# A bias table of 23 rows a head written by one transfer, decay read back two steps behind its store, and empty steps between gate and state steps

## The chip, the cores and the metric

The kernel runs on one core of a Trainium2 chip. The metric is the device time of one execution in microseconds (us), the median of several. The engines are TensorE (PE in the profile), VectorE (DVE), ScalarE (ACT), GpSimd (POOL) and SyncE (SP), which here only issues DMAs. Each engine works through its own instructions in order. DMAs are issued by SP and, for stores of projections, by ScalarE.

## The reference

One layer of a hybrid encoder for two groups of requests that share weights: a prompt of 2048 tokens and 8 samples of 16 tokens each. With D = 1024, 8 attention heads of 64 and 4 memory heads of 128:

```python
h = rms_norm(x, norm_g[0])
z = h @ w_in
qa, ka, va, qb, kb, vb, ob, ib, fb = jnp.split(z, IN_SPLITS, axis=-1)
...
idx = jnp.clip(q_pos[:, None] - k_pos[None, :], -REL_CLIP, REL_CLIP) + REL_CLIP
s = s + rel_table[:, idx]                 # chunk-band attention
...
b = jnp.cumsum(lf, axis=-1)               # mLSTM block of 64 tokens
m_t = jnp.maximum(b + m_prev, jnp.max(d_mat, axis=-1))
decay = jnp.exp(b[..., -1] + m_prev - m_new)
c_new = decay[..., None, None] * c_prev + jnp.einsum('bhs,bhsd,bhse->bhde', w_s, k, v)
...
x = x + rms_norm(jnp.concatenate([att, mlstm_out], axis=-1) @ w_out, norm_g[1])
x = x + rms_norm(conv_ffn(rms_norm(x, norm_g[2])), norm_g[3])
```

The bias of attention depends on the distance of query and key alone, so one row of 767 numbers per head holds all that is needed; the row of a query is that row shifted by one.

## The kernel before

All products run in float32 as three passes: each operand is split into a high and a low part, and `mm3` (L95, L96, L97) adds high by high and the two mixed products. A cast on ScalarE makes the high part, a subtraction on VectorE the low one.

The program has these stages, by time in the trace. Until about 1040 us the projection by w_in runs on TensorE, group by group: qk and qb (queries and keys, transposed, stored by L247), va and vo (values, by rows). The copies L232 and L234 on ScalarE take a finished accumulator out of PSUM, and TensorE needs them before it uses the accumulator again. Beside it run two side streams, attention (`att_stream`) and the memory heads (`mem_stream`). From about 1040 to 1300 us comes the product with w_out (`project`; wo is w_out scaled by gatt, L956). Then comes the FFN in a form with fewer products: up-projections (uec, ua, ub), convolution and gate, down-projections (dn and dnm with the halves wdh and wdl of weights and gh and gl of the gated activations). The down stage at about 2175 to 2300 us (names with 1_) has the preparation of rows of h2 interleaved.

A side stream is a `Pipe` of units. A unit is a Python generator that emits instructions up to its next `yield`; the two numbers of a yield are estimates of TensorE and VectorE time. `Pipe.step` starts one new unit and lets every live unit advance by one yield. `pump` is called between the matmuls of a projection and takes up to two such steps, turn and turn about between the pipes, as long as VectorE's estimated share is under 0.615 of the clock. `bubble()` is a unit with no instructions: a step in which only the units already live advance. So a `yield 0.0, 0.0` inside a unit puts distance between its two sides, and a bubble puts distance between two units.

What is emitted is then ordered anew by a scheduler, which simulates a timeline and may move instructions of one engine past each other where data allow it; only what stands in `keep_in_program_order` stays in its order against others of that kind. Tiles come from pools with a fixed number of buffers, and a load into a buffer waits until the last reader of the former content is done. DMAs share eight semaphores, so an issue waits until the DMA eight before it has landed.

The parts that the change touches:

- `build_bias` (L299): a row of 767 numbers for each head (ext) is written to DRAM, and from it the table relrow, in DRAM too, is filled (L310). `load_head` (L333) reads a tile nb of 128 shifted rows for each head and every second key group by `bias_src`; `queries` (L838) reads 16 shifted rows for the samples. A tile is read with a row step of SQ - 1 (SQ is 767), so row p starts p elements earlier.
- `load_head` also loads queries and keys of one head (qraw L342, kraw L345) and casts them (L350, L354).
- `prep_prompt` (L555, once for each half of the prompt) and `prep_sample` (L599) work out the gates: cumulative sums, maxima, and a pack pk of weights. They store the maxima (md, L590; mds, L631) and the decays (dd, L591; dds, L632) to DRAM and read the decays back spread over 128 partitions (dec, L593; decs, L634).
- `mlstm` (L665) loads pairs of chunks (mb from md, L672) and works through them; `mlstm_sample` (L734) takes 8 samples' states in four batches of two for each head: load cs (L777), matmuls cus (L789, L790), update, store (L795). cs has two buffers.
- `attention_sample` (L827) loads cached keys and values in pieces (skr L855, svr L905) through a pool of three raw buffers, casts them (skh L860, svh L909) and subtracts (skl L861, svl L910) for the products ss and sot.

Of the kernel before, what the change touches and what calls it, by code (L numbers as in the profile page):

```python
# [17 lines left out]
P = 128  # L18
# [26 lines left out]
def hymba_step(ctx: ExitStack, tc: tile.TileContext, I: dict, O: dict):  # L45
# [14 lines left out]
    def ps_sm(name):  # L60
        return psum.tile([P, 512], F32, tag="sm", name=name)

    def dt_(shape, name):
        return dram.tile(shape, F32, tag=name, name=name)
# [99 lines left out]
    def bubble():  # L164
        return iter([])
# [119 lines left out]
                    nc.scalar.dma_start(out[s - 3][:, 0 if s == 4 else t % 4, :], stage[:, :256])  # L285


    relrow = dt_([HA, P, SQ], "relrow")

    def raw_tile(name):  # L290
        return pa.tile([P, LS], F32, tag="raw", name=name, bufs=3)
# [7 lines left out]
    def build_bias():  # L299
        ext = dt_([HA, SQ], "ext")  # L300

        def unit():
            far, near = raw_tile("relf")[:HA, :383], rel[0]
            nc.vector.tensor_scalar(near, near, -1.0, None, op0=ALU.mult)
            nc.vector.tensor_copy(far, near[:, 0:1].broadcast_to([HA, 383]))
            nc.sync.dma_start(ext[:, 383:SQ], near)
            nc.sync.dma_start(ext[:, 0:383], far)
            yield 0.0, 0.75
            for h in range(HA):
                tc.keep_in_program_order(nc.sync.dma_start(relrow[h], ext[h:h + 1, :].broadcast_to([P, SQ])))  # L310
                yield 0.0, 0.0
                if h % 2:
                    yield 0.0, 0.0

        yield unit()
        yield FLUSH

    def bias_src(h, rows, cols):
        base = relrow[h]
        return bass.AP(base.tensor, base.offset + 127, [[SQ - 1, rows], [1, cols]])  # L320


    vhl = {}
# [231 lines left out]
    def prep_prompt(half):  # L555
        n = 8
        ig, lf, nlf = log_gates(1 + 8 * half, n, f"p{half}")
        f2 = lambda t: t.rearrange("p c h -> p (c h)")
        yield 0.3, 0.8
        a, b = cum_rows(f2(ig), f2(lf), f2(nlf), 32, tri, f"p{half}")  # L560
        ca = pm.tile([P, P], F32, tag="kw", name=f"cm{half}", bufs=2)[:32, :]
        nc.vector.tensor_tensor_scan(ca, a, a, NEG, op0=ALU.max, op1=ALU.max)
        yield 0.3, 0.4
        rt = ps_sm(f"rt{half}")
        transpose(rt[0:1, 0:32], ca[:, P - 1:P], 32)
        transpose(rt[0:1, 32:64], b[:, P - 1:P], 32)
        row = pm.tile([1, 2, n, HB], F32, tag="rowl", name=f"rowl{half}", bufs=1)
        nc.vector.tensor_copy(row.rearrange("p a c h -> p (a c h)"), rt[0:1, 0:64])
        o = 8 * half
        for h in range(HB):  # L570
            nc.vector.tensor_tensor_scan(mrow[:, o + 1:o + 9, h], row[:, 0, :, h], row[:, 1, :, h],
                                         mrow[:, o:o + 1, h], op0=ALU.max, op1=ALU.add)
        yield 0.3, 0.5
        mp = ps_sm(f"mp{half}")
        transpose(mp[0:32, 0:1], mrow[:, o:o + 8, :].rearrange("p c h -> p (c h)"), 1)
        mprev = small.tile([32, 1], F32, tag="mprev", name=f"mprev{half}")
        nc.vector.tensor_copy(mprev, mp[0:32, 0:1])
        yield 0.3, 0.8
        pk = pm.tile([P, P], F32, tag="kw", name=f"pk{half}", bufs=2)
        nc.vector.tensor_scalar(ca, ca, mprev, None, op0=ALU.max)  # L580
        nml = small.tile([32, 1], F32, tag="nml", name=f"nml{half}")
        nc.vector.tensor_scalar(nml, ca[:, P - 1:P], -1.0, None, op0=ALU.mult)
        nc.vector.tensor_copy(pk[0:32, :], a)
        nc.scalar.activation(pk[32:64, :], ca, AF.Exp, bias=mprev, scale=-1.0)
        nc.vector.tensor_tensor(b, b, ca, op=ALU.add)
        nc.scalar.activation(pk[64:96, :], b, AF.Exp, scale=-1.0)
        nc.scalar.activation(pk[96:128, :], a, AF.Exp, bias=nml)
        md = dt_([32, P], f"md{half}")
        dd = dt_([32, 1], f"dd{half}")
        nc.sync.dma_start(md, ca)  # L590
        nc.sync.dma_start(dd, pk[32:64, P - 1:P])  # L591
        dec = pm.tile([P, n, HB], F32, tag="dec", name=f"dec{half}", bufs=1)
        nc.sync.dma_start(dec, dd.rearrange("(c h) o -> o c h", c=n).broadcast_to([P, n, HB]))  # L593
        yield 0.0, 0.8
        cols = pack_columns(pk, "p")
        stab[half] = (md, dec, cols)
        yield 0.3, 0.8

    def prep_sample():  # L599
        ig, lf, nlf = log_gates(0, 1, "s")  # L600
# [6 lines left out]
        f2 = lambda t: t.rearrange("p c h -> p (c h)")  # L607
        a, b = cum_rows(f2(ig), f2(lf), f2(nlf), HB, trib, "s")
        yield 0.3, 0.8
        ms = small.tile([HB, DB], F32, tag="mss", name="mss")  # L610
        nc.sync.dma_start(ms, I["state_m"])
        ca = pm.tile([P, P], F32, tag="kw", name="cms", bufs=2)[:HB, :]
# [18 lines left out]
        nc.sync.dma_start(md, ca)  # L631
        nc.sync.dma_start(dd, v3(pk[32:32 + HB, :])[:, :, DS - 1])  # L632
        dec = pm.tile([P, HB, DB], F32, tag="decs", name="decs", bufs=1)
        nc.sync.dma_start(dec, dd.unsqueeze(0).broadcast_to([P, HB, DB]))  # L634
        yield 0.0, 0.8
        cols = pack_columns(pk, "s")
        stab["s"] = (md, dec, cols)
        yield 0.3, 0.8


    def finish_heads(num, enm, og, h, nch, dst, name):
# [92 lines left out]
    def mlstm_sample(h):  # L734
# [72 lines left out]
            yield bubble()  # L807
        for bp in range(DB // 2):
            yield batches(bp)
        yield finish()  # L810
        yield FLUSH

# [1075 lines left out]
```

## Time and profile before

| | us |
|---|---|
| median of 3 runs (2784.17 to 2784.3) | 2784.17 |
| the profiled execution | 2787.38 |
| its span | 2785.7 |

| engine | busy, share of the span |
|---|---|
| TensorE, matmuls | 97% |
| TensorE, weight loads | 91% |
| VectorE | 70% |
| ScalarE | 51% |
| GpSimd | 16% |

The mean granted clock of TensorE is 0.994 of full speed. In rows of the trace an instruction stands with its start, its duration, its engine, its line and the tiles it writes and reads; in square brackets is how long its engine stood idle before it and what ended that. SPq and ACTq are DMA issues of SP and ScalarE. In a table by stretches come the stretch, its length, the busy time and count of TensorE's matmuls and weight loads, VectorE, ScalarE and GpSimd, then the granted clock, the busy share of the 16 DMA engines and GB/s. A line of waits has the total, the number and the longest.

### The profile page before, as it was taken

To read this page: it belongs to the slowest core of one execution; us is meant where nothing else is said; L and a number is where in the kernel's file an instruction comes from. 1 tells how busy PE (TensorE), PEld (TensorE's weight loads), DVE (VectorE), ACT (ScalarE), POOL (GpSimd) and SP (SyncE) were. 2 spreads that over 40 slices of the span, in tenths; PEclk is the share of its full clock that TensorE was granted. 3 is DMA by queue.
4 is the path that set the end of the run, shared out by engine and by line. 5 is a ranking of instruction groups with operands and counts; after the bars stand their busy time and mean duration, and the time that the engine had idled before them with its cause. 6 is when DMAs were issued, how large, how long until landed. Compare 5 with 4: busy or idle time off the path is not lost.

```text
span 2785.7 us, 47226 instructions
## 1 busy us (share of the span) xinstructions
PE 2710.7 (97%) x16488; PEld 2536.9 (91%) x16488; DVE 1937.1 (70%) x3562; ACT 1422.1 (51%) x2871; POOL 445.9 (16%) x876
## 2 busy tenths in 40 slices
PE   7999999999999999999999999999999899999998
PEld 7899999998899998878999998799999778999877
DVE  5344455656456668766999988658888786888865
ACT  4355555635356666543554455445545565555543
POOL 1000010212000002244211110111111221222221
PEclk9999999999999999999999999999999999999999
DMA  5544355556555455355644459855555796555595
GB/s 182 158 122 133 104 180 160 169 156 213 157 170 149 143 171 177 111 178 179 217 169 169 167 167 323 295 174 170 177 171 171 252 344 223 169 176 182 177 320 191
DMA packets 334317, 516.35 MB, mean 185 GB/s; under 512 B 57122, under 2 KB 162558, under 8 KB 333950
## 3 DMA queue, kind: packets, MB, share of 16 engines
q1 hardware_dynamic: 295486, 479.49, 53.1%
q10 hardware_dynamic: 38592, 33.83, 3.6%
q8 instruction: 130, 2.13, 0.3%
q14 instruction: 109, 0.89, 0.1%
HBM read 371.61 MB, written 144.72 MB: 185 GB/s over the span
## 4 chain that ended last, share of the span: by engine, by line
PE 50%; DVE 4%; DMA 3%; issue 1%; POOL 1%; ACT 1%; SPq 0%; DVEq 0%; POOLq 0%; ACTq 0%
PE uec L95 6%; PE uec L96 6%; PE uec L97 6%; PE dn L97 3%; PE dn L95 3%; PE dn L96 3%; PE ua L97 3%; PE ua L96 3%; PE ua L95 3%; PE dnm L97 2%; PE dnm L95 2%; PE dnm L96 2%; PE wo L95 2%; PE wo L96 2%; PE wo L97 2%
## 5 line engine op out<-in xcount | busy, mean ns | idle before, releaser
L95 PE MATMUL uec<-B,wuh 128*128 128x384 f32 (+1 forms) x720 | 234.5, 328 | 3.1 <-DVE uu L1490 1.8
L96 PE MATMUL uec<-B,wuh 128*128 128x384 f32 (+1 forms) x720 | 235.1, 327 | 0.0
L97 PE MATMUL uec<-B,wul 128*128 128x384 f32 (+1 forms) x720 | 234.2, 327 | 0.0
L1283 ACT CAST wuh<-wu 128x512 fp32r<-128x512 f32 x255 | 141.7, 617 | 113.6 <-PE uec L96 102.8
L95 PE MATMUL dn<-wdh,gh 128*128 128x512 f32 x444 | 175.4, 395 | 5.6 <-ACT gh L1283 3.0
L96 PE MATMUL dn<-wdl,gh 128*128 128x512 f32 x444 | 175.7, 396 | 0.0
L1284 DVE TENSOR_TENSOR wul<-wu,wuh 128x512 fp32r<-128x512 f32 x255 | 165.1, 683 | 3.3 <-DMA x2d<-mx 3.3
L97 PE MATMUL dn<-wdh,gl 128*128 128x512 f32 x444 | 165.7, 399 | 0.8 <-DVE gl L1284 0.8
L401 DVE CUSTOM_DVE_ANT_0 tmp<-s,nb 128x640 f32<-128x640 f32 (+4 forms) x128 | 94.4, 737 | 97.7 <-PE s L391 95.8
L95 PE MATMUL vo<-wi_h,hT_c 128*128 128x256 f32 x544 | 155.9, 287 | 0.7 <-DVE mt L201 0.6
L97 PE MATMUL vo<-wi_h,hT_c 128*128 128x256 f32 x544 | 156.1, 287 | 0.0
L96 PE MATMUL vo<-wi_l,hT_c 128*128 128x256 f32 x544 | 155.4, 286 | 0.0
L95 PEld LDWEIGHTS uec<-B,wuh 128*128 128x128 f32 x720 | 134.9, 188 | 5.3 <-DVE uu L1490 2.4
L95 PE MATMUL qk<-hT_c,wi_h 128*128 128x384 f32 (+1 forms) x384 | 129.0, 336 | 6.9 <-ACT qk_st L232 4.2
L96 PEld LDWEIGHTS uec<-B,wuh 128*128 128x128 f32 x720 | 135.3, 188 | 0.2
L97 PEld LDWEIGHTS uec<-B,wul 128*128 128x128 f32 x720 | 135.1, 188 | 0.0
L414 DVE TENSOR_TENSOR ptl<-pt,pth 128x640 fp32r<-128x640 f32 (+4 forms) x128 | 93.6, 737 | 57.3 <-ACT pth L413 56.2
L1283 ACT CAST gh<-gr 128x768 fp32r<-128x768 f32 (+3 forms) x92 | 65.1, 719 | 132.0 <-PE dn L96 111.1
L402 ACT ACTIVATE tmp<-tmp,mn 128x640 f32<-128x640 f32 (+4 forms) x128 | 97.6, 763 | 64.7 <-DVE mn L401 62.2
L96 PE MATMUL qk<-hT_c,wi_h 128*128 128x384 f32 (+1 forms) x384 | 128.3, 334 | 0.0
L97 PE MATMUL qk<-hT_c,wi_l 128*128 128x384 f32 (+1 forms) x384 | 128.0, 333 | 0.0
L96 PE MATMUL qb<-hT_c,wi_h 128*128 128x384 f32 (+1 forms) x384 | 127.8, 333 | 0.0
(440 smaller groups left out, 8987.6 us busy)
## 6 DMA issues: line engine op xcount, KB each, us to landing
wu<-in_w_up SPq DMA_DIRECT2D x220, 256.0 KB, 3.7
wu<-wsd SPq DMA_DIRECT2D x176, 256.0 KB, 3.5
wdr<-in_w_down SPq DMA_DIRECT2D x121, 256.0 KB, 5.5
wi_raw<-in_w_in SPq DMA_DIRECT2D x52, 512.0 KB, 4.4
wsd<-ws SPq DMA_DIRECT2D x88, 256.0 KB, 3.0
gr<-gd SPq DMA_DIRECT2D x39, 384.0 KB, 4.2
kraw<-kTd SPq DMA_DIRECT2D x112, 128.0 KB, 3.1
gr<-gd SPq DMA_DIRECT2D x39, 320.0 KB, 5.2
```

The lines of the kernel that those rows point to most:

```text
L95: nc.tensor.matmul(out, ah, bh, start=start, stop=False, skip_group_check=onto)
L96: nc.tensor.matmul(out, ah, bl, start=False, stop=False, skip_group_check=onto)
L97: nc.tensor.matmul(out, al, bh, start=False, stop=stop, skip_group_check=onto)
L401: nc.vector.tensor_tensor_reduce(o_, s_, b_, 1.0, 3e38, ALU.add, ALU.min, accum_out=mn)
L402: nc.scalar.activation(tmp[:, :n], tmp[:, :n], AF.Exp, bias=mn, scale=-1.0, accum_out=rsum[:, i % 4, hh:hh + 1])
L414: nc.vector.tensor_tensor(s.ptl[:, sl, qc], ptv, s.pth[:, sl, qc], op=ALU.subtract)
L1283: nc.scalar.copy(h, r)
L1284: nc.vector.tensor_tensor(l, r, h, op=ALU.subtract)
```

## The change

The table relrow gets 16 + 128/16 - 1 = 23 equal rows a head in place of 128, written by one transfer for all heads. A bias tile of 128 rows is read as 8 groups of 16 rows: inside a group a row starts one element earlier than the one above, and a group starts one table row less 16 elements later, so the values are the same. The steps of `build_bias` fall from one for each transfer and four empty ones to one. The read-backs of decay move to the end of the gate preparation, two yields and some behind their stores, and are kept in program order. Empty yields follow the yields of `prep_prompt` and most of those of `prep_sample`, and a bubble follows each of the four state batches of a head.

```diff
-    relrow = dt_([HA, P, SQ], "relrow")
+    REL_ROWS = 16 + P // 16 - 1
+    relrow = dt_([HA, REL_ROWS, SQ], "relrow")
...
             yield 0.0, 0.75
-            for h in range(HA):
-                tc.keep_in_program_order(nc.sync.dma_start(relrow[h], ext[h:h + 1, :].broadcast_to([P, SQ])))
-                yield 0.0, 0.0
-                if h % 2:
-                    yield 0.0, 0.0
+            tc.keep_in_program_order(
+                nc.sync.dma_start(relrow, ext.unsqueeze(1).broadcast_to([HA, REL_ROWS, SQ])))
+            yield 0.0, 0.0
...
         base = relrow[h]
-        return bass.AP(base.tensor, base.offset + 127, [[SQ - 1, rows], [1, cols]])
+        step = [[SQ - 1, rows]] if rows <= 16 else [[SQ - 16, rows // 16], [SQ - 1, 16]]
+        return bass.AP(base.tensor, base.offset + 127, step + [[1, cols]])
...
         yield 0.3, 0.8
+        yield 0.0, 0.0
         a, b = cum_rows(f2(ig), f2(lf), f2(nlf), 32, tri, f"p{half}")
...
         nc.sync.dma_start(dd, pk[32:64, P - 1:P])
         dec = pm.tile([P, n, HB], F32, tag="dec", name=f"dec{half}", bufs=1)
-        nc.sync.dma_start(dec, dd.rearrange("(c h) o -> o c h", c=n).broadcast_to([P, n, HB]))
         yield 0.0, 0.8
+        yield 0.0, 0.0
         cols = pack_columns(pk, "p")
         stab[half] = (md, dec, cols)
         yield 0.3, 0.8
+        yield 0.0, 0.0
+        tc.keep_in_program_order(
+            nc.sync.dma_start(dec, dd.rearrange("(c h) o -> o c h", c=n).broadcast_to([P, n, HB])))
+        yield 0.0, 0.0
...
         for bp in range(DB // 2):
             yield batches(bp)
+            yield bubble()
         yield finish()
```

`prep_sample` gets the same edits for decs. Lines of the changed kernel are 1 to 13 higher than those of before.

What the scheduler makes of it, at three places. First SP's issues between 59 and 90 us, from the table of biases to the first keys. Before:

```order
L310 DMA relrow_358<-ext_982 128x767 x4
L333 DMA nb0_0_1288<-relrow_358 128x640
L333 DMA nb1_0_1359<-relrow_358 128x640
L1169 DMA wi3_raw0_1209<-in_w_in1 128x1024
L310 DMA relrow_358<-ext_982 128x767 x2
L342 DMA qraw0_0_1292<-qTd0_0_94 64x512
L619 DMA out_m_sample<-mnew_950 4x8
L631 DMA mds_962<-cms_947 4x128
L632 DMA dds_963<-pks_953 32x1x1
L342 DMA qraw0_0_1292<-qTd0_0_94 64x512
L634 DMA decs_966<-dds_963 128x32
L345 DMA kraw0_0_0_1293<-kTd0_0_78 64x512 x2
```

And in the changed kernel:

```order
L311 DMA relrow_358<-ext_945 184x1x767
L333 DMA nb0_0_1174<-relrow_358 128x1x640
L342 DMA qraw0_0_1178<-qTd0_0_94 64x512
L1182 DMA wi3_raw0_1172<-in_w_in1 128x1024
L342 DMA qraw0_0_1178<-qTd0_0_94 64x512
L333 DMA nb1_0_1249<-relrow_358 128x1x640
L640 DMA mds_982<-cms_967 4x128
L628 DMA out_m_sample<-mnew_970 4x8
L641 DMA dds_983<-pks_973 32x1x1
L649 DMA decs_986<-dds_983 128x32
L345 DMA kraw0_0_0_1179<-kTd0_0_78 64x512 x2
```

The queries moved up to the table; the read-back of decs still follows its store, and the keys follow it.

The second place is around 720 to 737 us, where the samples' attention takes its seventh batch (names with 6) while the prompt's second half is prepared (md1, dd1, dec1). SP before:

```order
L855 DMA skr6_0_9219<-in_cache_k 128x512
L855 DMA skr6_1_9248<-in_cache_k 128x512
L590 DMA md1_8501<-cm1_8396 32x128
L591 DMA dd1_8502<-pk1_8492 32x1
L672 DMA mb0_8_10371<-md1_8501 128x2x128
L593 DMA dec1_8505<-dd1_8502 128x32
L855 DMA skr6_2_9277<-in_cache_k 128x512
L855 DMA skr6_3_9309<-in_cache_k 128x512
L905 DMA svr6_0_9362<-in_cache_v 128x512
```

And in the changed kernel:

```order
L868 DMA skr6_0_9211<-in_cache_k 128x512
L675 DMA mixs_166<-nums3_8417 128x128
L868 DMA skr6_1_9240<-in_cache_k 128x512
L1290 DMA out_m_prompt<-mrow_367 1x4
L868 DMA skr6_2_9270<-in_cache_k 128x512
L868 DMA skr6_3_9302<-in_cache_k 128x512
L918 DMA svr6_0_9355<-in_cache_v 128x512
L594 DMA md1_9140<-cm1_8944 32x128
L595 DMA dd1_9141<-pk1_9131 32x1
L684 DMA mb0_8_10364<-md1_9140 128x2x128
```

ScalarE at the same place, before:

```order
L584 ACTIVATE pk1_8492<-cm1_8396,mprev1_8468 32x128
L860 CAST skh6_0_9257<-skr6_0_9219 128x528
L860 CAST skh6_1_9287<-skr6_1_9248 128x528
L587 ACTIVATE pk1_8492<-ap1_8393,nml1_8494 32x128
L909 CAST svh5_4_9225<-svr5_4_9196 16x512
```

And in the changed kernel:

```order
L873 CAST skh6_0_9249<-skr6_0_9211 128x528
L247 DMA qTd3_2_111<-qk3_1_st0_1_9221 128x128
L247 DMA qTd3_3_112<-qk3_1_st0_1_9221 128x256
L922 CAST svh5_4_9217<-svr5_4_9184 16x512
L873 CAST skh6_1_9280<-skr6_1_9240 128x528
```

All loads of skr moved ahead of the stores md1 and dd1 and of mb, which reads md1; the cast of svr5_4, whose buffer skr6_2 takes, moved ahead of that of skr6_1.

The third place is in the down stage around 2218 us: weights wdr with their halves wdh and wdl, gated activations gq with gh and gl, rows f13 of the result. ScalarE before, and then VectorE before:

```order
L1283 CAST wdh1_5_25058<-wdr1_5_0_25060 128x512
L1107 CAST B4_2_24858<-b2112_25105 128x4x128
L1283 CAST wdh1_5_25058<-wdr1_5_1_25064 128x512
L1283 CAST gh1_10_25165<-gq1_10_25017 128x768
L1283 CAST wdh1_5_25058<-wdr1_5_2_25068 128x512
```

```order
L1284 TENSOR_TENSOR wdl1_5_25059<-wdr1_5_0_25060,wdh1_5_25058 128x512
L1108 TENSOR_TENSOR B4_2_24858<-b2112_25105,B4_2_24858 128x4x128
L1284 TENSOR_TENSOR wdl1_5_25059<-wdr1_5_1_25064,wdh1_5_25058 128x512
L1446 SCALAR_TENSOR_TENSOR f13_25096<-f13_25096,drs3_21354,norm_row3_16271 128x512
L1284 TENSOR_TENSOR gl1_10_25166<-gq1_10_25017,gh1_10_25165 128x768
```

In the changed kernel, ScalarE and then VectorE:

```order
L1296 CAST wdh1_5_25051<-wdr1_5_0_25053 128x512
L1296 CAST gh1_10_25158<-gq1_10_25010 128x768
L1296 CAST wdh1_5_25051<-wdr1_5_1_25057 128x512
L1125 COPY b2112_25098<-h2T_pt12_0_1_25093 128x512
L1296 CAST wdh1_5_25051<-wdr1_5_2_25061 128x512
```

```order
L1297 TENSOR_TENSOR wdl1_5_25052<-wdr1_5_0_25053,wdh1_5_25051 128x512
L1297 TENSOR_TENSOR gl1_10_25159<-gq1_10_25010,gh1_10_25158 128x768
L1297 TENSOR_TENSOR wdl1_5_25052<-wdr1_5_1_25057,wdh1_5_25051 128x512
L1459 SCALAR_TENSOR_TENSOR f13_25089<-f13_25089,drs3_21347,norm_row3_16264 128x512
L1147 TENSOR_TENSOR t412_25100<-h2T_pt12_0_1_25093,t212_25041 128x512
```

The activations of the step moved ahead of its second weight piece, and on VectorE ahead of the row f13.

More of the change, by code (lines that the diff above doesn't have):

```diff
@@ L592, in prep_prompt @@
         dec = pm.tile([P, n, HB], F32, tag="dec", name=f"dec{half}", bufs=1)
-        nc.sync.dma_start(dec, dd.rearrange("(c h) o -> o c h", c=n).broadcast_to([P, n, HB]))
         yield 0.0, 0.8
+        yield 0.0, 0.0
         cols = pack_columns(pk, "p")
@@ L597, in prep_prompt @@
         yield 0.3, 0.8
+        yield 0.0, 0.0
+        tc.keep_in_program_order(
+            nc.sync.dma_start(dec, dd.rearrange("(c h) o -> o c h", c=n).broadcast_to([P, n, HB])))
+        yield 0.0, 0.0
     def prep_sample():
@@ L609, in prep_sample @@
         yield 0.3, 0.8
+        yield 0.0, 0.0
         ms = small.tile([HB, DB], F32, tag="mss", name="mss")
@@ L633, in prep_sample @@
         dec = pm.tile([P, HB, DB], F32, tag="decs", name="decs", bufs=1)
-        nc.sync.dma_start(dec, dd.unsqueeze(0).broadcast_to([P, HB, DB]))
         yield 0.0, 0.8
+        yield 0.0, 0.0
         cols = pack_columns(pk, "s")
@@ L638, in prep_sample @@
         yield 0.3, 0.8
+        yield 0.0, 0.0
+        tc.keep_in_program_order(nc.sync.dma_start(dec, dd.unsqueeze(0).broadcast_to([P, HB, DB])))
+        yield 0.0, 0.0
     def finish_heads(num, enm, og, h, nch, dst, name):
```

## The prediction

> **What bounds the kernel now.** The page first, then the busy time by stretches, then TensorE's waits.
>
> ```profile
> span 2785.7 us, 47226 instructions
> PE 2710.7 (97%) x16488; PEld 2536.9 (91%) x16488; DVE 1937.1 (70%) x3562; ACT 1422.1 (51%) x2871; POOL 445.9 (16%) x876
> ```
>
> TensorE is busy for 2710.7 of 2785.7 us, so at most 75 us are idle, and the change takes no large matmul away. All it can do is move idle stretches and the clock dips that go with them. The stretches show where the idle time is:
>
> ```profile
> 45.00:130.00 85.00, 75.72 (x481) 72.09 (x481) 31.55 (x105) 28.09 (x67) 2.43 (x8) 1.00 0.55 163
> 130.00:520.00 390.00, 390.00 (x2828) 385.19 (x2828) 201.43 (x456) 204.89 (x479) 22.77 (x72) 1.00 0.45 137
> 520.00:760.00 240.00, 227.63 (x1530) 214.05 (x1530) 135.33 (x394) 109.44 (x283) 40.34 (x122) 0.98 0.58 178
> 760.00:1030.00 270.00, 269.88 (x2085) 266.90 (x2084) 163.33 (x376) 163.86 (x395) 15.35 (x50) 1.00 0.52 156
> 1030.00:1170.00 140.00, 136.32 (x829) 119.22 (x828) 108.31 (x227) 86.11 (x222) 38.26 (x64) 0.99 0.49 154
> 2200.00:2300.00 100.00, 93.53 (x413) 74.01 (x412) 81.68 (x118) 61.67 (x112) 23.09 (x21) 0.98 0.93 320
> 736.00:743.00 7.00, 6.08 (x23) 6.08 (x24) 3.42 (x6) 3.36 (x7) 0.50 (x2) 0.51 0.60 176
> 1043.00:1047.00 4.00, 3.41 (x18) 3.32 (x18) 3.81 (x10) 3.00 (x7) 0.99 (x3) 0.57 0.86 280
> 2220.00:2225.00 5.00, 3.92 (x11) 3.11 (x12) 5.00 (x7) 3.85 (x8) 3.79 (x4) 0.66 0.77 256
> ```
>
> The first two figures of a row are the stretch and its length, the third is TensorE's busy time, and the one after POOL is the granted clock. From 130 to 520 and from 760 to 1030 nothing is idle: there the change has nothing to win. It can win in four places: 9.3 us are idle before 130, 12.4 between 520 and 760, 3.7 around 1040 and 6.5 after 2200. The last three rows show the clock falling after idle stretches. Lost time there is length times (1 - clock): 3.4 us at 736, 1.7 at 1043, 1.7 at 2220, all counted as busy. The order of both kernels is the same up to 57 us, from 740 to 1040 and from 1170 to 2207 apart from line numbers; only these four places can differ.
>
> **The table of biases (59 to 112 us).** Eight transfers go, one comes.
>
> ```profile
> L310 SPq DMA_DIRECT2D relrow<-ext x8: 475/548/604, 59.4 to 99.2; - x8
> 74.50 0.79 SPq L632 DMA_DIRECT2D dds<-pks  x1
> 76.21 0.51 SPq L342 DMA_DIRECT2D qraw<-qTd  x1
> 81.02 0.35 SPq L634 DMA_DIRECT2D decs<-dds  x1
> 81.27 0.62 ACT L350 CAST qs<-qraw 128x512 fp32r<-128x512 f32 x1 [8.90 <-DMA kTd<-qk_st]
> PE qk L95 <- ACT qk_st L232: 4.2, 2, 2.5
> PE qk L95 <- ACT qk_st L234: 1.9, 1, 1.9
> ```
>
> Eight transfers of 128x767 floats are 3.14 MB; one of 184x767 is 0.56 MB. At 163 GB/s, the last figure of the first stretch above, the 2.57 MB less are some 16 us of DMA. What TensorE sees of that is smaller. ScalarE stood 8.90 us before the cast of qraw at 81.27, whose second half SP issued only at 76.21, and the copy that TensorE needs (L232) stood behind that cast. TensorE's waits for ScalarE here are 4.2 + 1.9 = 6.1 us. In the order of the changed kernel qraw stands right behind relrow, so the wait at 82 should go, and the later two may shrink. But decs is still issued directly behind dds, and SP stood there from 74.50 + 0.79 to 81.02, with kraw queued behind it. That wait does not move (the read-back two steps on was put back next to its store by the scheduler), and it delays kraw as before. Bounds: -6.1 if all goes, +2.0 if kraw stays late and the casts now ahead of the copies wait instead (the size of the 1.9 wait). I take **-4.3**, about two thirds of the 6.1, nearest to the rows of the waits behind qraw.
>
> The transfer changes shape, too. A bias tile (nb) is read through two levels, 8 by 16 rows.
>
> ```profile
> DMA to landing us min/median/max: 2.9/4.2/5.5
> PE s L391: 95.8, 54
> POOL nb L334: 401.3, 15
> ```
>
> Its 16 loads land in 4.2 us (median). VectorE's bias step (L401) sits idle 95.8 us for scores of TensorE; no wait for the bias is listed. GpSimd's 401.3 us for the loads are time in which it has nothing else to do. So I cost a longer load at nothing; that cover is gone if loads are so slow that SP stops for a lane.
>
> [...]
>
> **The read-backs of decay and the stop at 737.** Three DMAs move behind their stores. That of decs was dealt with above. The prompt's first (dec0) stood 3.3 us on SP for its store, and stands behind two mb and a vraw now; no wait of TensorE ends there: 0. The second (dec1) was in this piece of the trace:
>
> ```profile
> SPq L593 <- DMA dd<-pk: 3.3, 1, 3.3
> 723.74 1.22 SPq L591 DMA_DIRECT2D dd<-pk  x1
> 728.94 0.38 SPq L672 DMA_DIRECT2D mb<-md  x1
> 729.95 0.85 SPq L855 DMA_DIRECT2D skr<-in_cache_k  x2
> 726.21 0.63 ACT L860 CAST skh<-skr 128x528 fp32r<-128x528 f32 x1 [1.84 <-DMA skr<-in_cache_k]
> 727.95 0.68 DVE L910 TENSOR_TENSOR svl<-svr,svh 16x512 fp32r<-16x512 f32 x1 [0.36 <-ACT svh L909]
> 736.24 0.63 ACT L860 CAST skh<-skr 128x528 fp32r<-128x528 f32 x1 [7.58 <-DMA skr<-in_cache_k]
> 736.92 0.59 PE L95 MATMUL ss<-skh,zhl 128*128 128x264 f32 x1 [3.05 <-ACT skh L860]
> DMA to landing us min/median/max: 2.6/3.2/6.2
> ```
>
> SP stood at mb for md's landing (728.94); skr of batch 6 left only at 729.95 and took 6.2 us, the longest of its kind, so TensorE stood 3.05 us and then ran at half clock. Its buffer came free behind svl (727.95 + 0.68), which stood behind a cast that waited for another load (726.21). So two things must move. In the changed order both do: all four loads of skr stand ahead of md, dd and mb on SP, and the cast svh5_4 stands ahead of skh6_1 on ScalarE. Casting svh5_4 at about 724, behind skh6_0, frees the buffer some 2 to 3 us sooner; with the 1.3 us from 728.63 to 729.95 the load starts some 3.5 to 5 us sooner, which covers the 3.05. Queued behind md now: mb0_8, mb0_10 and then svr6_1, whose product TensorE reaches some 75 projection matmuls later. Bounds: -6.4 (3.05 + 3.4 of half clock), and 0 if the load is still late. I take **-6.4**.
>
> [...]
>
> **The state batches.** An empty step follows each of 16.
>
> ```profile
> PE cus L789 <- DMA cs<-in_state_c: 4.2, 5, 1.9
> 559.72 0.34 SPq L795 DMA_DIRECT2D out_c_sample<-cs  x1
> 564.33 0.33 SPq L777 DMA_DIRECT2D cs<-in_state_c  x1
> ```
>
> Five batches make TensorE wait 4.2 us: two buffers, and a load that SP issues when the store of the batch before last has landed (559.72 to 564.33). In the new order the load still stands directly behind that store, and the four batches of a head stand 16, 22 and 32 projection matmuls apart where they stood 15, 28 and 33, in the next head 27, 9 and 32 for 15, 12 and 43. The scheduler takes the empty steps up, and what one batch gains another gives back: **0**, between -2 and +2 (half of the 4.2 either way).
>
> **Around 1041 and 2218.** These move because the scheduler counts time onward.
>
> ```profile
> PE mT_pt L67 <- ACT vo_st L232: 1.0, 1, 1.0
> 1039.97 1.33 ACT L956 ACTIVATE wo<-wor,gatt 128x512 fp32r<-128x512 f32 x2 [1.99 <-DMA wor<-in_w_out]
> 2215.08 0.62 ACT L1283 CAST wdh<-wdr 128x512 fp32r<-128x512 f32 x1 [1.85 <-DMA wdr<-wtd]
> 2217.19 0.83 ACT L1283 CAST gh<-gq 128x768 fp32r<-128x768 f32 x1
> 2219.41 0.75 DVE L1446 SCALAR_TENSOR_TENSOR f<-f,drs,norm_row 128x512 f32<-128x512 f32 x1 [1.40 <-DMA f<-f1d]
> 2218.07 0.50 PE L95 MATMUL dnm<-wdh,gh 128*128 128x512 f32 x1 [2.15 <-ACT gh L1283]
> 2221.08 0.79 PE L97 MATMUL dnm<-wdh,gl 128*128 128x512 f32 x1 [1.84 <-DVE gl L1284]
> ```
>
> At 1041 the copy vo_st stood behind two casts that waited 1.99 us for a weight; in the new order it stands ahead of them. -1.0 for the wait, -1.7 for the dip at 1043 if it goes; bounds -2.7 and 0, I take **-2**. At 2218 gh1_10 stood behind two casts and gl1_10 behind a row that waited for f1d until 2219.41. In the new order gh1_10 stands directly behind the cast of 2215.08 and gl1_10 ahead of the row with f1d, so gh would be ready at about 2215.1 + 0.6 + 0.8 = 2216.5 and TensorE, idle since 2215.9, would wait 0.6 or 0.7 of the 2.15 + 1.84 = 4.0 us. That is -3.3, and -1.7 more if the dip at 2220 goes: bounds -5.0 and 0, I take **-4**, the dip gone in part.
>
> **New stalls.** Between 57 and 740 the order is dealt anew. Before, this stretch held 9.3 + 12.4 us of idle time, of which 6.1, 4.2 and 3.05 are dealt with above; the other 8 us are coincidences, and about half as much may come anew: **+4**, between 0 and +8.
>
> **Sum.** -4.3 - 6.4 + 0 - 2 - 4 + 4 = -12.7 us. The profiled execution took 2787.38 us, which gives 2774.7; the runs' median lies 3.2 below it (2784.17), so 2771.5 is what runs should show. With all low bounds 2762, with all high ones 2796.
>
> **Rivals.** (1) *The stop at 737 only moves.* If skr still lands late (it took 6.2 us once, 3.2 mostly), 6.4 come back: 2778. For it: the buffer, not SP's order, was the last thing. Against: the new row on ScalarE. (2) *No net gain.* The stalls are coincidences of two pipes with a projection, and a new deal has as many: early gain -4.3 against +4 to +8 of new stalls, with nothing at 737, 1041 and 2218 but other gaps: 2782 to 2788, taken 2784. The unmoved decs and the empty steps taken up speak for it: of what the change says, only the smaller table then acts. (3) *Slower: the bias loads.* If nb takes twice its 4.2 us, the two loads of the first heads hold lanes in front of qraw and kraw, +8.4, with a dip of 3.4: +11.8 in place of -4.3. With nothing gained at 737 that is 11.8 - 2 - 4 + 4 = +9.8: 2794. It decides from the point at which a load ends later than SP needs its lane, eight transfers on; that VectorE's bias step waits for scores and not for nb speaks against it. [...]
>
> **How the numbers follow.** Chances: forecast 0.52, rival 1 0.22, rival 2 0.19, rival 3 0.07. 0.2% (5.6 us) is about what a measurement can tell from no change: 2778.6 and 2789.7. Faster takes nearly all of the forecast, three quarters of rival 1 and little of rival 2: 0.69; slower is rival 3 and a little: 0.08; the rest 0.23. The range leaves out rival 3, the upper end of rival 2 and the lowest bounds: 2763 to 2785.
>
> **What would show it.** One relrow row landing before 70 us and no wait of qk for L232 at 82; decs still right behind dds; skr of batch 6 issued before md and no gap above 1 us at 737, with the clock there at 1.0; cus still waiting some 4 us; gh1_10 ahead of its second cast, with less than 1.5 us of gaps around 2218. Wrong: the sum fails if the idle time between 57 and 740 is again above 20 us, or if nb loads land above 8 us with SP waiting behind them.

## The result, and the profile after

| | before | changed |
|---|---|---|
| median of 14 runs (us) | 2784.24 (2779.23 to 2792.54) | 2793.78 (2784.75 to 2800.62) |
| the profiled execution (us) | 2787.38 | 2792.38 |
| its span (us) | 2785.7 | 2789.6 |

The ratio is 1.0026, 95% interval 1.0014 to 1.0037: slower by about 7 us, where 13 us less were forecast. Single executions of the changed kernel lie up to 16 us apart, so a profile shows where time goes, and the ratio how much.

The page and the stretches of the changed kernel, in the columns of before:

```profile
span 2789.6 us, 47201 instructions
PE 2712.1 (97%) x16488; PEld 2539.5 (91%) x16488; DVE 1935.2 (69%) x3562; ACT 1419.0 (51%) x2871; POOL 448.3 (16%) x876
45.00:130.00 85.00, 78.62 (x489) 75.94 (x488) 35.31 (x116) 32.62 (x79) 3.26 (x9) 0.96 0.44 133
520.00:760.00 240.00, 229.63 (x1601) 218.16 (x1600) 138.84 (x408) 112.28 (x295) 40.62 (x125) 1.00 0.60 181
1030.00:1170.00 140.00, 134.51 (x821) 118.60 (x820) 107.14 (x229) 85.80 (x220) 37.36 (x62) 0.98 0.53 154
2200.00:2300.00 100.00, 92.94 (x406) 72.22 (x406) 81.77 (x116) 60.36 (x110) 27.61 (x23) 0.98 0.94 316
77.00:84.00 7.00, 5.42 (x18) 5.42 (x19) 0.98 (x2) 2.42 (x6) 0.29 (x2) 0.51 0.18 52
384.00:391.00 7.00, 7.00 (x25) 5.78 (x26) 3.38 (x7) 2.24 (x6) 1.60 (x4) 0.52 0.91 262
736.00:743.00 7.00, 7.00 (x48) 6.96 (x47) 1.48 (x3) 1.33 (x3) 0.82 (x2) 1.00 0.30 98
1046.00:1050.00 4.00, 3.89 (x20) 3.65 (x20) 3.93 (x12) 3.51 (x10) 0.89 (x2) 0.57 0.87 275
1084.00:1088.00 4.00, 4.00 (x19) 3.92 (x20) 2.94 (x8) 2.15 (x5) 0.90 (x2) 0.57 0.99 319
2258.00:2262.00 4.00, 3.74 (x16) 2.99 (x17) 3.57 (x6) 2.00 (x6) 0.97 (x2) 0.57 0.91 254
```

Before 130 TensorE is busier by 2.9 us, but the clock is at 0.51 from 77 to 84, where before had full speed. At 736 the clock is whole now. Dips now stand at 384, 1046, 1084 and 2258. Where the time goes is best read by taking the same product (the n-th matmul of the same projection) in both traces and subtracting its starts. This difference, worked out from the starts of the two traces, grows or falls so:

| stretch (time in before) | changed minus before at its end, us | gained or lost in it |
|---|---|---|
| up to 52 (same order in both) | +1.2 | +1.2 |
| 52 to 132 | +2.9 | +1.7 |
| 132 to 703 | +5.4 | +2.5 |
| 703 to 743 | -0.1 | -5.5 |
| 743 to 1028 | +2.4 | +2.5 |
| 1028 to 1130 | +6.5 | +4.1 |
| 1130 to 2157 | +3.5 | -3.0 |
| 2157 to 2238 | -0.4 | -3.9 |
| 2238 to 2279 | +3.1 | +3.5 |
| to the end | +4.0 | +0.8 |

Two of the forecast gains are there, 5.5 us up to 743 and 3.9 us at 2218. The one before 130 is a loss, the stretch with the one at 1041 loses 4.1, and what came at 2218 was given back 20 us later. In the stretch before 130 the rows of SP, ScalarE and TensorE are these:

```profile
60.66 0.78 SPq L311 DMA_DIRECT2D relrow<-ext  x1
69.17 0.62 SPq L333 DMA_DIRECT2D nb<-relrow  x1
69.89 0.51 SPq L342 DMA_DIRECT2D qraw<-qTd  x1
71.06 0.48 SPq L342 DMA_DIRECT2D qraw<-qTd  x1
76.92 0.62 ACT L350 CAST qs<-qraw 128x512 fp32r<-128x512 f32 x1 [9.41 <-DMA qraw<-qTd]
77.56 0.97 ACT L637 ACTIVATE pks<-pks 4x128 f32<-4x128 f32 x3
78.58 0.48 PE L67 MATMUL pkTs<-ident,pks 128*128 128x128 f32 x1 [3.88 <-ACT pks L637]
```

The one transfer of 0.56 MB took 8.5 us (60.66 to the issue of nb at 69.17, which waited for it). The queries stand behind nb, the cast of the queries stands ahead of the exponentials pks, and TensorE stood 3.88 us for these, with 6.8 us at half clock.

### The profile page after: what moved, and what is told of

It is laid out like the page before. It is cut to its first block, busy times and chain, and to the rows that moved or that the text cites. A ratio compares the mean times of both kernels' runs of the same rounds, so it can differ in the third digit from the quotient of the medians.

```text
span 2789.6 us, 47201 instructions
## 1 busy us (share of the span) xinstructions
PE 2712.1 (97%) x16488; PEld 2539.5 (91%) x16488; DVE 1935.2 (69%) x3562; ACT 1419.0 (51%) x2871; POOL 448.3 (16%) x876
## 4 chain that ended last, share of the span: by engine, by line
PE 54%; DVE 4%; DMA 4%; issue 1%; ACT 1%; POOL 1%; SPq 0%; DVEq 0%; POOLq 0%; ACTq 0%
PE uec L95 6%; PE uec L96 6%; PE uec L97 6%; PE dn L97 3%; PE dn L95 3%; PE dn L96 3%; PE ua L97 3%; PE ua L96 3%; PE ua L95 3%; PE dnm L97 2%; PE dnm L95 2%; PE dnm L96 2%; PE wo L95 2%; PE wo L97 2%; PE wo L96 2%; PE ub L96 1%
```

## The experiments

Theory T held that the small table is what costs: its transfer, or the loads from it. Theory D held that any change of the steps deals the work anew and the stops fall elsewhere. Every ratio is to the kernel before, with its 95% interval.

**The parts alone.** The first has the table's three edits alone. The second has the gate steps and read-backs alone, the third the bubbles alone:

```diff
             yield batches(bp)
+            yield bubble()
```

The fourth is the full change with the table's edits undone.

> The kernel before with the small table alone (one transfer of 23 rows a head, read through two levels, one step in place of twelve). Theory T (the table is the loss): SP stands behind the one transfer for some 8.5 us, the queries land at about 77 us, ScalarE's cast of them stands ahead of the exponentials of the gates and of the copy that TensorE needs, so TensorE stands 3 to 4 us near 78 and runs at half clock for 6.8 us (3.4 lost); the time is 4 to 8 us over before. Theory D (a new deal: any change of the steps re-places all work between 57 and 740 us and the stops fall elsewhere): the stop at 78 may come too, but the time is anywhere from -6 to +6, and the stops between 350 and 740 us are not those of the full change.

> The kernel before with the empty steps of the gate preparation and the moved read-backs alone (table with 128 rows, no bubbles between state batches). Theory T: no stop near 78 us, the wait of 3.3 us of SP for the first decay is gone, and the stop of 3.05 us at 737 is gone as in the full change, since the load of the cached keys stands ahead of the gate stores: 4 to 8 us under before. Theory D: -6 to +6, with new stops of 1 to 4 us somewhere between 130 and 740 us that before does not have.

> The kernel before with the bubble after each state batch alone. Theory T: nothing changes before the first state batch (about 410 us), the waits of cus for cs stay between 2 and 6 us (4.2 in before), the time is within 3 us of before. Theory D: the stops after 410 us are dealt anew and the time is anywhere from -6 to +6.

> The full change without the table (its gate steps, read-backs and bubbles). Theory T: the full change's loss goes and the gain at 737 stays: 5 to 9 us under the full change, 0 to 4 us under before. Theory D: its time is no sum of the parts; it lies within 6 us of before, and the stops of the full change at 382 (1.3 us with half clock) and at 1046 and 1083 are not all there though this part of the code is the same.

| kernel | ratio | interval |
|---|---|---|
| small table alone | 1.0039 | 1.0025 to 1.0053 |
| gate steps and read-backs alone | 1.0077 | 1.0060 to 1.0094 |
| bubbles alone | 1.0113 | 1.0099 to 1.0128 |
| full change without the table | 1.0097 | 1.0084 to 1.0110 |

The table alone did what theory T said, with a stop of 4.67 us at 83, though it cost some 11 us and not 4 to 8. The rest went against T and beyond D's bounds: the parts are all slower than the whole, and they do not add up. In the kernel with bubbles alone TensorE stood here, and this is its stretch beside that of before (columns as above):

```profile
1228.61 1.11 PE L1096 MATMUL h2T_pt<-ident,x2r 128*128 128x128 f32 x4 [6.18 <-DVE x2r L1088]
1240.18 1.11 PE L67 MATMUL mT_pt<-ident,mr 128*128 128x128 f32 x4 [4.62 <-DVE mr L994]
1215.00:1250.00 35.00, 22.26 (x92) 17.84 (x92) 21.27 (x21) 12.98 (x25) 14.14 (x19) 0.71 0.61 191
```

```profile
1205.00:1240.00 35.00, 30.01 (x137) 24.06 (x136) 22.20 (x23) 16.58 (x34) 17.48 (x25) 0.90 0.63 213
```

TensorE is busy 22 us in place of 30, at a clock of 0.71. Before this place the two kernels' difference is +4.6 us, behind it +20.0. Counting matmuls of wo in the traces, the last product of attention starts after 381 of them in before and in the full change, after 408 in the third and fourth kernels; the last of the memory heads after 252 and 255 as against 312. In the third and fourth the side streams end late, and the last rows of the w_out stage and the first of the FFN then have no cover. The second, with the gate steps alone, is another case: its streams end after 384 and 286, and its trace, of the slowest of its six executions, is 25 us behind before's on both sides of this place. It loses them earlier (18 us behind at 550, 11 at 1028, 25 at 1200), and what they go to was not tried.

**Steps or shape.** The fifth issues the eight large transfers in one step, so that its steps are those of the small table. The sixth adds one empty step to before. The seventh writes the table by rows and then by heads, 32 rows each:

```diff
-    REL_ROWS = 16 + P // 16 - 1
+    REL_ROWS = 32
...
-                nc.sync.dma_start(relrow, ext.unsqueeze(1).broadcast_to([HA, REL_ROWS, SQ])))
+                nc.sync.dma_start(relrow.rearrange("h r c -> r h c"),
+                                  ext.unsqueeze(0).broadcast_to([REL_ROWS, HA, SQ])))
```

The eighth has that and reads a bias tile in 16 groups of 8 rows; the addresses are the same bytes:

```diff
-        step = [[SQ - 1, rows]] if rows <= 16 else [[SQ - 16, rows // 16], [SQ - 1, 16]]
+        step = [[SQ - 1, rows]] if rows <= 16 else [[SQ - 8, rows // 8], [SQ - 1, 8]]
```

> The kernel before with one edit: its eight transfers of the bias table are issued in one step, and the eleven empty steps behind them go. So the steps are placed as with the small table alone, but the table has its 128 rows. Theory T (the table's transfer is the loss): no stop of 4 us near 80 us, ScalarE copies for TensorE ahead of the cast of the queries; -4 to +2 against before. Theory D (the deal of steps is the loss): about what the small table alone cost, +5 to +15, most of it behind 100 us and around 540 to 560.

> The kernel before with one more empty step behind the table: no work is added or taken. Theory T: within 2 us of before. Theory D: the attention pipe starts one step later, orders change, and the time moves by 3 us or more, more likely up than down, since the order of before has fewer stops than those of the first four kernels.

> The full change with a table of 32 rows a head, written by one transfer that goes by rows and then by heads (0.79 MB in place of 0.56). If the shape of the transfer made it slow, it lands in 3 to 6 us (8.5 in the full change), and since the exponentials of the gates now also stand ahead of the cast of the queries on ScalarE, the stop of 3.88 us at 78 and its half clock of 3.4 go: 4 to 7 us under the full change, 0 to 3 over before. If size or waiting made it slow, it lands in 8.5 us or later and the stop stays. Theory D: the rest of the stops (382, 500 to 515, 1046, 1083) stays, as the plan of steps is that of the full change.

> As the one with 32 rows, and a bias tile is read as 16 groups of 8 rows in place of 8 groups of 16. If the bias loads of the full change are slow and matter, they land sooner (4.2 us, the median of before, in place of some 5.5) and the time falls by another 1 to 4 us. If they are hidden, within 2 us of the one with 32 rows.

| kernel | ratio | interval |
|---|---|---|
| large table in one step | 1.0004 | 0.9993 to 1.0014 |
| one more empty step | 1.0002 | 0.9993 to 1.0011 |
| full change, 32 rows | 1.0017 | 1.0006 to 1.0027 |
| full change, 32 rows, 16 groups | 0.9983 | 0.9973 to 0.9993 |

Theory D in its general form falls: eleven steps fewer, or one more, move the time by nothing that can be measured. The shape of the transfers does move it. The seventh alone is not clear: it was expected 4 to 7 us under the full change, and 1.0017 against 1.0026 is 2.5 us with intervals that overlap. The seventh and the eighth have the same order of instructions on every engine and differ by 0.34%, about 9 us, in favour of the eighth, which is faster than before; 1 to 4 us were expected. The early rows of the eighth:

```profile
59.65 0.68 SPq L311 DMA_DIRECT2D relrow<-ext  x1
66.65 0.58 SPq L334 DMA_DIRECT2D nb<-relrow  x1
70.11 0.97 ACT L638 ACTIVATE pks<-pks 4x128 f32<-4x128 f32 x3 [3.76 <-DVE pks L633]
74.61 0.62 ACT L351 CAST qs<-qraw 128x512 fp32r<-128x512 f32 x1 [3.53 <-DMA qraw<-qTd]
45.00:130.00 85.00, 80.94 (x529) 78.15 (x528) 38.89 (x123) 34.71 (x84) 3.11 (x9) 1.00 0.50 147
```

A table of 0.79 MB landed in 7.0 us, 112 GB/s, where 0.56 MB had taken 8.5 us, 66 GB/s. The landing came less early than was expected, but the stop at 78 and its dip are gone: 80.94 us busy of 85 at full clock. The earlier landing is not shown to be the reason: ScalarE's order differs too, and pks, for which TensorE stood at 78 in the full change, now runs at 70.11, ahead of the cast of the queries (74.61) in place of behind it.

**One number, and the rest of the change.** The ninth is the full change with the second of these edits alone. The tenth is the full change with the large table in one step. The eleventh is before with the fast form of the table alone, the twelfth the full change with the fast form and without the bubbles.

> The full change with one number changed: a bias tile is read as 16 groups of 8 rows in place of 8 groups of 16 (the table keeps its 23 rows and its transfer). The kernel with 32 rows stood at 1.0017 of before, with 16 groups as well at 0.9983. If the 16 bias loads are what costs (theory B), the full change falls from 1.0026 to 0.999 to 1.0005, with the stop near 78 us still there, as the table's transfer and the order are those of the full change. If only table and loads together matter, or the earlier step was chance, it stays between 1.0015 and 1.004.

> The full change with the table of 128 rows, its eight transfers issued in one step: gate steps, read-backs and bubbles as in the full change, steps as in the full change, the only thing undone is the small table. The fourth kernel had the same with eleven empty steps more behind the table, stood at 1.0097, and its two side streams ran out 27 and 60 products of the w_out stage later than before. Here they run out where they do in before. If that is what the fourth lost (theory S, a late end of the side streams), this one stands at 0.997 to 1.001; if the empty steps in gates and states cost by themselves, at 1.005 to 1.010.

> The kernel before with the small table alone, in the form with 32 rows written by rows and read in 16 groups of 8 (one step). With 23 rows and 8 groups of 16 this stood at 1.0039. Theory B (the shape of the table's transfer and of the loads costs): 0.997 to 1.001, no stop above 2 us near 80. If the change of the order by the table costs, 1.002 to 1.005 again.

> The full change without the bubbles behind the state batches, the table in the form with 32 rows and 16 groups of 8. With bubbles it stood at 0.9983. If the bubbles neither cost nor bring anything as long as the side streams run out in time (here they do), within 0.1% of that: 0.997 to 0.9995. If they bring something, 1.000 or above.

| kernel | ratio | interval |
|---|---|---|
| full change, 16 groups of 8 | 0.9999 | 0.9987 to 1.0011 |
| full change, large table in one step | 0.9994 | 0.9985 to 1.0004 |
| fast table alone | 1.0006 | 0.9997 to 1.0015 |
| fast table, gates, no bubbles | 0.9986 | 0.9976 to 0.9996 |

The ninth has the order of the full change on every engine, row by row, and stands 0.27% under it, some 7.5 us, with the stop near 78 still there (4.25 us). Where this comes from can be followed in the two traces. A weight wor for the w_out product is issued right behind a bias load; the rows are SP's, ScalarE's and TensorE's, in the full change and then in the ninth:

```profile
1036.70 0.63 SPq L333 DMA_DIRECT2D nb<-relrow  x1
1037.43 0.39 SPq L959 DMA_DIRECT2D wor<-in_w_out  x1
1043.32 0.72 ACT L969 ACTIVATE wo<-wor,gatt 128x512 fp32r<-128x512 f32 x1 [2.98 <-DMA wor<-in_w_out]
1045.73 0.38 PE L706 MATMUL ms<-mqk 128*128 128x128 f32 x1 [2.85 <-DVE num L724]
```

```profile
1034.21 0.55 SPq L333 DMA_DIRECT2D nb<-relrow  x1
1034.88 0.52 SPq L959 DMA_DIRECT2D wor<-in_w_out  x1
1039.22 0.72 ACT L969 ACTIVATE wo<-wor,gatt 128x512 fp32r<-128x512 f32 x1 [1.37 <-DMA wor<-in_w_out]
1041.65 0.38 PE L706 MATMUL ms<-mqk 128*128 128x128 f32 x1 [1.14 <-DVE num L724]
```

The weight arrives 5.9 us after its issue in the one and 4.3 us in the other; behind its cast on ScalarE waits num, and behind that TensorE, 2.85 us against 1.14, and in the full change the clock falls at 1046. By the starts of the same products the full change loses 3.2 us to the ninth here, 3.2 us more around the next bias load (1066), 2.4 us between 480 and 520, about the load at 490, and 2.9 us around 385, where no bias load is near and only one of them has the dip. In other stretches it gains some back; at the end of the traces 6.5 us are left.

At 1066 the way goes through GpSimd. There the norm's factor n_rs stands behind the step that waits for nb, and VectorE waits for n_rs. From VectorE the delay reaches TensorE through ScalarE. GpSimd, VectorE and TensorE, in the full change and then in the ninth:

```profile
1073.93 0.14 POOL L334 MEMSET nb<- 64x64 f32 x1 [1.11 <-DMA nb<-relrow]
1075.34 1.28 DVE L1047 SCALAR_TENSOR_TENSOR mx<-mx,n_rs,norm_row 128x1024 f32<-128x1024 f32 x1 [2.22 <-POOL n_rs L84]
1082.78 0.38 PE L426 MATMUL ot<-pth,vhl 128*128 128x256 f32 x1 [1.53 <-ACT pth L413]
```

```profile
1066.89 0.14 POOL L334 MEMSET nb<- 64x64 f32 x1 [0.99 <-DMA nb<-relrow]
1068.42 1.31 DVE L1047 SCALAR_TENSOR_TENSOR mx<-mx,n_rs,norm_row 128x1024 f32<-128x1024 f32 x1 [0.84 <-POOL n_rs L84]
1075.63 0.39 PE L426 MATMUL ot<-pth,vhl 128*128 128x256 f32 x1 [0.64 <-ACT pth L413]
```

The delay is not that of these loads alone. A transfer's landing can be taken from the updates of its semaphore in the trace: it is the last update before the next transfer on that semaphore. Counted so for all 16 bias loads, with the same transfers compared in the full change and the ninth kernel, and in the seventh and eighth, a load takes 1.3 and 1.5 us longer (mean) with 8 groups; the transfer issued next on SP takes 1.1 us longer in both, the fourth behind the load still 0.7 and 0.9, the sixth 0.0 and 0.1.

The tenth answers the other question: without the small table, gate steps, read-backs and bubbles together make no difference (0.9994), and the eleven empty steps behind the table that it lacks against the fourth kernel decide whether the side streams end in time (381 and 252 here) or late. The eleventh shows that the fast form takes the loss of the table alone (1.0039) away, and the twelfth that the bubbles do nothing as long as the streams end in time (0.9986 without, 0.9983 with).

**What was still open.** The pair that follows has a table of 144 rows a head, in eight transfers, and one order of instructions; it differs in the grouping of the read alone:

```diff
-    relrow = dt_([HA, P, SQ], "relrow")
+    relrow = dt_([HA, 144, SQ], "relrow")
...
+        step = [[SQ - 1, rows]] if rows <= 16 else [[17 * SQ - 16, 8], [SQ - 1, 16]]
...
+        step = [[SQ - 1, rows]] if rows <= 16 else [[9 * SQ - 8, 16], [SQ - 1, 8]]
```

The last is the bubbles with the fast form of the table and without gate steps.

> The kernel before with a table of 144 rows a head (eight transfers, twelve empty steps as before), and a bias tile read as 8 groups of 16 rows, 17 table rows apart less 16 elements. The order of instructions is the same in this kernel and the next one; they differ in the grouping of the read alone, bytes and addresses' spacing inside a row being equal. Theory B (a read whose outer count is 8 is slow and delays what stands behind it): this one is 3 to 8 us (0.1 to 0.3%) over the next, and the profile shows no landing for its transfers, as in the full change. If the read's shape does not matter, the two lie within 1.5 us.

> The same as the one before it, the bias tile read as 16 groups of 8 rows, 9 table rows apart less 8 elements. Theory B: 3 to 8 us under the one before it and within 4 us of the kernel before; landings of the bias loads shown, at 3 to 7 us.

> The kernel before with the table of 32 rows read in 16 groups of 8 and the bubbles behind the state batches, without gate steps and moved read-backs. In its order the side streams run out after 408 and 312 matmuls of the w_out stage (381 and 255 in the full change). Theory S (a late end of the side streams is what made the parts alone slow): 1.006 to 1.013, with a stop of 4 to 7 us and half clock of 15 us or more around 1220 to 1245 us, though the table is in the fast form. If the slow parts were slow for the slow table transfers' sake, 0.998 to 1.002.

| kernel | ratio | interval |
|---|---|---|
| 144 rows, 8 groups of 16 | 1.0082 | 1.0065 to 1.0099 |
| 144 rows, 16 groups of 8 | 1.0073 | 1.0045 to 1.0102 |
| fast table and bubbles | 1.0118 | 1.0102 to 1.0135 |

The pair's medians are 2806.93 and 2801.95 us, but by the ratios the difference is 0.09% with wide intervals, so this pair alone does not settle the size. One of the six executions of the second took 2825.03 us, at a mean granted clock of 0.926 (0.990 to 0.993 in all others); the other five have a mean of 2800.7 us, 0.23% under the 2807.1 of the first. With 8 groups a bias load takes 1.5 us longer here too, and the next transfer 1.2. The pair has the same mark at the same place, again first with 8 groups and then with 16:

```profile
1051.68 0.72 ACT L957 ACTIVATE wo<-wor,gatt 128x512 fp32r<-128x512 f32 x1 [3.55 <-DMA wor<-in_w_out]
1054.10 0.80 PE L695 MATMUL ms<-mqk 128*128 128x128 f32 x2 [3.43 <-DVE num L713]
```

```profile
1047.90 0.72 ACT L957 ACTIVATE wo<-wor,gatt 128x512 fp32r<-128x512 f32 x1 [1.95 <-DMA wor<-in_w_out]
1050.32 0.49 PE L695 MATMUL ms<-mqk 128*128 128x128 f32 x2 [1.85 <-DVE num L713]
```

Both kernels of the pair are 0.7 to 0.8% slower than before, where the second was expected within 4 us. 9 and 7 us of that are lost before 132 us in their traces, and their streams end as in the full change (381 and 255). Their table has an eighth more rows and is read in two levels, and the order differs from that of before; which of these costs was not separated.

The last kernel did what its order said: streams that end after 408 and 312 matmuls of wo, a stop of 6.38 us at 1240, 17 us of half clock there, 1.0118. A table in the fast form does not help it. At that place it falls back by 15 us, as the third and fourth kernels do; in all, the three traces end 35, 20 and 25 us behind before's. So the late end of the streams costs some 15 us in these three kernels, and the order shows it ahead of a run. It is not what the gate steps alone, the small table alone or the pair above lose by.

## Why the prediction was wrong

**The bias loads.** The step that failed is "So I cost a longer load at nothing; that cover is gone if loads are so slow that SP stops for a lane." The row on which it rested was true, VectorE's bias step waited for scores and not for nb, but it asks the wrong question. The load is paid for by the transfers behind it: a weight 1.6 us later, and TensorE's wait 1.7 us longer through ScalarE, with a dip behind. At 1066 it is paid for by GpSimd too, of which the prediction said that it has nothing else to do: n_rs stood behind the wait for nb. In three pairs of kernels with one order each the grouping measured 0.27%, 0.34% and (uncertain) 0.09%; the first two are 7.5 and 9 us, of the 20 between the forecast of -12.7 and the +7 that came. The median load took 5.7 us, and 3.9 before, by the semaphores (the 4.2 that the prediction took for 16 loads is the profile's figure for two of them). So neither sign that the prediction named for being wrong appeared: the longest load took 8.0 us, and the idle time between 57 and 740 was 18.7 us, as before (18.9). What the transfers behind a load lose was not on its list. The third rival named the loads, with 0.07, and put the cost in front of the first heads, where it is not. Its 2794 fits the 2793.78 by size, not by place.

An outer count of 16 in place of 8 is all that the ninth kernel changes, and the updates of the semaphores go with it. In the full change every bias load, read in 8 groups, has 9 updates, one 1.0 to 1.1 us after its issue and eight within the 0.2 to 1.7 us before it lands; read in 16 groups in the ninth kernel it has 16. Why a load in 8 groups takes longer was not shown. Nor does any run show the third rival's factor of two: a load took 5.7 us, against 4.3 in the ninth kernel and 3.9 in before.

**The table's transfer.** "In the order of the changed kernel qraw stands right behind relrow" overlooked nb between them, which waits for the table. With 8.5 us for 0.56 MB the cast of the queries still began 4.4 us earlier than before (76.92 against 81.27), but on ScalarE it had moved ahead of pks (70.89 in before, 77.56 now) and the copies, so TensorE's wait moved from 82 to 78 and a dip of 6.8 us came with it. This is the +2.0 end of that term, and the dip that it left out: +1.7 in place of -4.3. With 32 rows, and pks ahead of the cast again, it is a gain (-2.7 at 132 in the eighth kernel's trace).

**737.** Right: all loads of skr left ahead of md (729.82 against 732.13, below), no stop is left, and 703 to 743 gave 5.5 of the 6.4 us.

```profile
729.82 1.72 SPq L868 DMA_DIRECT2D skr<-in_cache_k  x2
732.13 0.35 SPq L594 DMA_DIRECT2D md<-cm  x1
PE cus L801 <- DMA cs<-in_state_c: 4.7, 3, 2.1
```

**The state batches.** Right: the last line, from the waits of TensorE between 520 and 760, has 4.7 us where 4.2 were, and the forecast was 0.

**1041.** The copy did move ahead of the two casts, and its wait is gone. What was late next is what the step should have named: num (L723) still stands behind the cast of wor, and wor stands behind nb. So by 1074 nothing is won (+0.6), and nearly all of the +4.1 comes between 1074 and 1082, behind the next bias load. The ninth kernel shows whose it is: there the stretch from 1028 to 1074 gains 2.6 us, where 2 were forecast, and the loss behind it is absent (-2.7 at 1090). From 1028 to 1090 the eighth gains 2.6 as well, and the seventh, with 8 groups, loses 3.2.

**2218.** The -4 came (-3.9), and +3.5 was lost within 20 us: the wait of h2T_pt at 2258 was 0.97 us and is 2.31 with a dip. The step priced the two rows that moved forward and nothing of what comes after them. What made that wait longer was not tried and stays open.

**New stalls.** +4 was put in for 57 to 740. Apart from the terms above that stretch lost 2.5, and another 2.5 came between 743 and 1028, where the order is the same and nothing was expected. From 132 to 703 the trace of the ninth kernel gains 0.5 and that of the eighth loses 4.7, both with 16 groups, so the read does not settle this stretch. Its cause stays open, and so does that of the second 2.5 (3.1 in the ninth).

**What is left of the forecast.** In the eighth kernel the bias loads are fast and the stop at 78 is gone, and it gains 0.17%, 4.7 us of the 12.7. So some 8 us of the forecast were missing for other reasons than these two.

## What to carry to other kernels

When a DMA is written with a new access pattern, look at its outer count before looking at the bytes: a single transfer of 0.56 MB took 8.5 us here, where four old ones of 0.39 MB each, side by side, had all landed 10.9 us after the first was issued, and one number (16 groups of 8 in place of 8 of 16) moved the time by 0.27 and 0.34%, as much as the whole change lost. A prefetch that no busy engine waited for had a price here all the same, namely what is queued behind it (a weight 1.6 us later); follow that transfer to its reader. And where empty steps pace side streams, count in the order where the streams end: ending 27 and 60 matmuls late cost 15 us in three kernels here.

## What the runs showed of the hardware

In the traces of before and of the full change the clock fell to half for 3.41 or 6.83 us at a time, apart from the fall at the very end, and in the last kernel for some 17 us around 1240 (a clock of 0.76 over the 35 us from 1227). It fell after short stops too: 1.31 us of waiting at 382 was followed by 6.83 us of it, and the 1.14 us at 1041 in the ninth kernel by none (a clock of 1.00 from 1036 to 1046).

In the trace of the full change 2049 of the 2074 transfers have 16 updates of their semaphore, and the 20 with an outer count of 8 (the bias loads, the table and three small ones) have 9. The table of 23 rows has one 1.2 us after its issue and eight from 66.15 to 69.15 us, the table of 32 rows in the eighth kernel sixteen, the last 7.0 us after its issue. The profile gives a landing only where a semaphore has 16 updates for each of its transfers: in before that holds for two of the eight semaphores, in the full change for none. So its figure for the time from issue to landing is that of a few transfers. Three rows of the lists of DMA issues, of before, of the full change and of the ninth kernel:

```profile
nb<-relrow SPq DMA_DIRECT2D x16, 320.0 KB, 4.2
```

```profile
nb<-relrow SPq DMA_DIRECT2D x16, 320.0 KB
```

```profile
nb<-relrow SPq DMA_DIRECT2D x16, 320.0 KB, 4.9
```

The last figure is the median of two loads of 16 in the first row and the third, and in the second, where the bias loads leave no semaphore with a whole count, it is missing. By all 16 loads the medians are 3.9, 5.7 and 4.3 us. The eighth kernel, with the table of 32 rows and 16 groups of 8, is the best found: 0.9983 of before, interval 0.9973 to 0.9993.
